# FFN chunks 2 to 10: first product made transposed, with weight blocks as stationary operands, and x^T scaled by the norm's factor

## The chip, the cores and the metric

One core of a Trainium2 chip runs the whole network. The metric is the device time of one launch in microseconds (us), the median of several runs. The engines named below are PE (matrix product; PEld is its weight load), DVE (vector), ACT (scalar), POOL and SP (which issues the weight DMAs). PE, ACT, DVE and POOL each run their own instructions in a fixed order and wait for one another by semaphores.

## What is computed

256 tokens of width 1024 pass through a first block of 4 layers and a second block of 2 layers. The FFN is the same gated product everywhere; there are 8 in the first block and 2 in the second, each with 2816 hidden values:

```python
def rms_norm(x, g, eps=NORM_EPS):
    xf = x.astype(jnp.float32)
    y = xf * lax.rsqrt(jnp.mean(xf * xf, axis=-1, keepdims=True) + eps)
    return (y * g.astype(jnp.float32)).astype(x.dtype)

def swiglu(x, w_in, w_out):
    gate, up = jnp.split(x @ w_in, 2, axis=-1)
    return (jax.nn.silu(gate) * up) @ w_out

    for i in range(DEPTH):
        g = norm_g[i]
        h = h + 0.5 * rms_norm(swiglu(rms_norm(h, g[0]), ffn_w_in[i, 0], ffn_w_out[i, 0]), g[1])
        m = rms_norm(h, g[2])
...
        h = h + rms_norm(m, g[3])
        h = h + 0.5 * rms_norm(swiglu(rms_norm(h, g[4]), ffn_w_in[i, 1], ffn_w_out[i, 1]), g[5])
```

The dots stand for an attention: differential in layers 0 and 3, causal in layer 1, and a three-branch one in layer 2. The second block's layers have a mixer and an FFN each, with norms that are shifted and scaled.

## The kernel before

The 256 tokens are two token tiles (t0 and t1) of 128 partitions, `h[0]` and `h[1]`. The network is 16 stages: in the first block FFN, attention, FFN for each layer (stages 0 to 11), then mixer and FFN twice (12 to 15). The ten FFNs are stages 0, 2, 3, 5, 6, 8, 9, 11, 13 and 15.

**Weights.** All weights are float32 and are read once. SP brings them as 128x2048 tiles `raw` (two buffers). Each is split (`hilo`) into a rounded part hi (ACT, CAST, L168) and a rest lo (DVE, subtraction, L169), in 128x1024 tiles, nine buffers of each. The activations are split in the same way, and a product is three matmuls (`mm3`): xh with wh (L217), xh with wl (L219), xl with wh (L221).

**An FFN** (`ffn`) goes over 11 chunks of 256 hidden columns. For a chunk c and a token tile t, `f1(c, t)` makes [tokens, 256 gate | 256 up] in one PSUM bank: `project`, 8 k-tiles of 3 matmuls, in which the stationary operand is a 128x128 block of x^T and the moving one is 512 columns of weights. `hidden` makes tanh (ACT, L411), the two products (DVE, L413, L414), and then `to_hT`: two PE transposes (L249), a cast (ACT, L261), a subtraction (DVE, L262). `f2(c, t)` multiplies these hidden values by rows of the second weight, into the accumulators aA (for t0) and aB (for t1), two banks each, 12 matmuls of 512 columns for a chunk and a token tile. The second product runs two chunks behind the first; after chunk 10 chunks 8, 9 and 10 are left for t0, then for t1.

**Between FFNs.** `finish` makes the sum of squares of the accumulator (ACT, L312; POOL, L313, L314), a power (POOL, L304), and adds to h (DVE, L379, L380). Then `prep` makes x^T for the next stage: the norm's factor r (again Square, L313, L314, L304) and, of it, r/2 and r^2 (POOL, L334, L335); the transposes of h (L249, two groups of four for each token tile); and with the norm's gain xh (ACT, L351) and xl (DVE, L352). The transposes take h as it is; r enters later, as r/2 in the tanh and as r^2 in L414. For the second block `prep_2` scales h by r on ACT (L1113) ahead of its transposes.

**Order.** Steps that hop between engines are generators that yield a number of us of PE's products, after which the next step is written; the framework then orders each engine's instructions by its own priorities, so that a group of transposes can stand between matmuls of another product.

Of the kernel before, what the change touches and what calls it, by code (L numbers as in the profile page):

```python
# [99 lines left out]
class _Net:  # L100
# [63 lines left out]
    # A float32 value is the exact sum of two float32r parts, hi and lo.  x @ w is taken as  # L164
    # xh @ wh + xh @ wl + xl @ wh, accumulated in float32.
# [69 lines left out]
    def out_step(self, acc, hT, ws, first, last, halves=(0, 1)):  # L235
        for k in range(2):
            x = ([hT[0][:, i] for i in range(2)], [hT[1][:, i] for i in range(2)])
# [3 lines left out]
    def last_steps(self, acc, steps):  # L241
        """steps: (hT, ws); one half of the columns after the other"""
# [8 lines left out]
    def to_hT(self, nat, scale=None):  # L251
        """[128 tok, 256] -> (hi, lo) [128, 2, 128 tok]."""
# [13 lines left out]
        return hi, lo  # L266

# [1 line left out]
    def setup(self):  # L269
# [13 lines left out]
        def columns(src, rows, eng=nc.sync):  # L283
            """DRAM [rows, 128] -> [128, rows]."""
# [14 lines left out]
        self.xT = [tuple(self.t(self.xp, [P, KT, P], f"x{n}{t}", F32R) for n in "hl") for t in range(NT)]  # L299

# [5 lines left out]
    def mean_square(self, halves, a0, a1):  # L306
        """a0 + a1 * the sum of squares of two [128, 512]; a1 is a number, a0 a number or [128, 1]"""
# [12 lines left out]
    def rstd(self, r, x):  # L320
        """r = (mean square of x [128, 1024] + eps) ^ -1/2"""
        self.powmh(r, self.mean_square(self.halves(x), EPS, 1.0 / D))

    def prep(self, t, li, slot):
        """x^T of the token tile with the norm's gain; gives the norm's factor per token (and
        half of it, and its square), which stays out of the products."""
        nc = self.nc
        h = self.h[t]
        fs = self.t(self.sp, [P, 3], f"fs{t}", bufs=2)

        def factors():
# [9 lines left out]
        yield 3.0 * t if initial else PREP_0  # L341
# [13 lines left out]
        if initial:  # L355
            factors()
        return fs
# [6 lines left out]
    def post_norm(self, t, acc, g_bc, a=1.0, eps=EPS):  # L364
        """h += acc * (a * mean square of acc + eps) ^ -1/2 * g"""
# [17 lines left out]
    def prepare(self, n, t):  # L383
        """Starts what the next part of the network needs of a token tile."""
# [12 lines left out]
    def ffn(self, w_in, w_out, factors, finish, middle):  # L397
# [3 lines left out]
        hT, wi, wo, acc = {}, {}, {}, {}  # L401

        def f1(c, t):
            self.prepared(t)
            if c not in wi:
                wi[c] = self.load_in(w_in, [(c * FC, FC), (DFF + c * FC, FC)])
            self.start(hidden(c, t, self.project(t, wi[c], 2 * FC)))

        def hidden(c, t, ps):
            th = self.t(self.fp, [P, FC], "th")  # L410
            nc.scalar.activation(th, ps[:, :FC], AF.Tanh, scale=factors(t)[0])  # L411
            hd = self.t(self.fp, [P, FC], "hd", bufs=3)
# [17 lines left out]

        first = ((0, 0), (0, 1), (1, 0), (1, 1)) if self.stage == 0 else ((0, 0), (1, 0), (0, 1), (1, 1))
# [17 lines left out]
    def ffn_1(self, li, j):  # L449
# [14 lines left out]
        self.ffn(self.a["ffn_w_in"][li, j], self.a["ffn_w_out"][li, j], factors, finish, middle)  # L464

# [1 line left out]
    def rope(self, x, nh, t):  # L467
        """first 16 of 64 dims of nh heads of x [128, nh, 64], in place"""
# [24 lines left out]
    def softmax(self, s, n, l):  # L493
        """s: PSUM [128, n, l] -> exp(s/8 - max) [128, n, l] and sums [128, n]"""
# [21 lines left out]
    def masked_scores(self, parts, dg):  # L516
        """parts: (psum slice, q^T, k^T) of a bank; dg: psum [128, n, 128], the diagonal blocks"""
# [11 lines left out]
    def qkv_layer(self, kind, w_in, w_out, li):  # L529
        """diff (kind 0) or plain causal (kind 1: with 256 tokens the one block of 256 is every  # L530
        query's own and none is left to select) attention."""
# [38 lines left out]
        def heads(j, t, pairs, last):  # L570
            """A group of pairs of 64-wide heads (or of diff heads of 2 components)."""
# [884 lines left out]
```

## Time and profile before

| | |
|---|---|
| runs | 2869.83, 2873.69, 2874.76 us |
| median | 2873.69 us |
| profiled execution, span | 2868.0 us |
| PE busy | 2823.5 us, 98%, 13373 matmuls |
| DVE, ACT, POOL busy | 66%, 53%, 8% |
| DMA | 549.32 MB, mean 192 GB/s |
| PE clock granted (mean) | 0.999 of full |

The span runs from the first to the last instruction of the profiled execution; the page gives no other time for that execution, and the median of the runs is 5.7 us above the span. On the page, an engine's share is its busy time by the span; the chain of waits is followed back from the last instruction; a row of the timeline is a start, a duration, the engine, the line, and the operation with output and inputs, and a bracket gives the idle time ahead of it and what ended it. A matmul's duration is longer than the distance to the next one, since they are pipelined, so distances of starts are used where PE's time is counted.

### The profile page before, as it was taken

What the parts mean: (1) busy time and instruction counts of PE and PEld (TensorE: products, weight loads), DVE (VectorE), ACT (ScalarE), POOL (GpSimd) and SP (SyncE); (2) the same over time, 40 slices, a digit from 0 to 9 for tenths busy, and PEclk for the clock granted to TensorE, in tenths of its full rate; (3) what the DMA queues carried; (4) which work ended last, traced back from release to release, by engine and by line L of the source; (5) the groups of instructions that cost most, each with busy time, mean ns of one, the idle gap of its engine ahead of it and who ended that gap; (6) DMA issues with size and microseconds to landing.
All of it is one profiled execution on the core that took longest, in us unless ns stands there. A gap on an engine that the chain in (4) does not pass through costs nothing.

```text
span 2868.0 us, 36025 instructions
## 1 busy us (share of the span) xinstructions
PE 2823.5 (98%) x13373; PEld 2311.4 (81%) x13373; DVE 1879.8 (66%) x2913; ACT 1509.0 (53%) x2655; POOL 231.5 (8%) x441
## 2 busy tenths in 40 slices
PE   8999999999999999999999999999999999999998
PEld 6887788888888888878888888778778888788787
DVE  6565767656466765656767666675676686675854
ACT  5456644545664454557545546654545544554543
POOL 0011200101110010020100001110001000000000
PEclk9999999999999999999999999999999999999999
DMA  7554567555446755552666555365565586564753
GB/s 236 186 181 157 171 219 243 179 188 187 157 158 217 249 182 180 191 157 74 222 211 220 194 181 188 128 227 191 187 203 201 172 294 202 192 223 168 236 182 126
DMA packets 356755, 549.32 MB, mean 192 GB/s; under 512 B 13890, under 2 KB 270772, under 8 KB 356580
## 3 DMA queue, kind: packets, MB, share of 16 engines
q1 hardware_dynamic: 354964, 542.00, 57.5%
q0 software_dynamic: 1248, 4.41, 0.4%
q8 instruction: 105, 1.72, 0.2%
q14 instruction: 70, 0.57, 0.1%
q10 hardware_dynamic: 368, 0.62, 0.1%
HBM read 545.93 MB, written 1.05 MB: 191 GB/s over the span
## 4 chain that ended last, share of the span: by engine, by line
PE 84%; ACT 4%; DVE 4%; DMA 4%; POOL 2%; issue 1%; SPq 0%; POOLq 0%; ACTq 0%; DVEq 0%
PE mm L221 18%; PE mm L217 17%; PE mm L219 17%; PE aA L217 4%; PE aA L219 4%; PE aA L221 4%; PE tp L249 4%; PE aB L221 3%; PE aB L217 3%; PE aB L219 3%; DVE lo L169 2%; ACT hi L168 1%; DMA raw<-in_ffn_w_in_dram 1%; DMA raw<-in_w_in_dram 1%; ACT junk L312 1%
## 5 line engine op out<-in xcount | busy, mean ns | idle before, releaser
L169 DVE TENSOR_TENSOR lo<-raw,hi 128x1024 fp32r<-128x1024 f32 x914 | 1102.1, 1221 | 668.1 <-ACT hi L168 655.7
L168 ACT CAST hi<-raw 128x1024 fp32r<-128x1024 f32 x914 | 942.8, 1049 | 927.6 <-PE mm L221 318.9
L217 PE MATMUL mm<-hi,xh 128*128 128x512 f32 (+2 forms) x2496 | 1005.2, 403 | 5.7 <-ACT hi L168 4.0
L221 PE MATMUL mm<-hi,xl 128*128 128x512 f32 (+2 forms) x2496 | 976.7, 392 | 4.3 <-DVE xl L352 4.3
L219 PE MATMUL mm<-lo,xh 128*128 128x512 f32 (+2 forms) x2496 | 973.0, 390 | 0.5 <-DVE lo L169 0.5
L221 PEld LDWEIGHTS mm<-hi,xl 128*128 128x128 f32 x2496 | 469.0, 188 | 108.6 <-DVE xl L352 8.1
L217 PEld LDWEIGHTS mm<-hi,xh 128*128 128x128 f32 x2496 | 469.7, 188 | 94.0 <-ACT hi L168 4.4
L219 PEld LDWEIGHTS mm<-lo,xh 128*128 128x128 f32 x2496 | 470.6, 189 | 87.6 <-DVE lo L169 1.0
L217 PE MATMUL aA<-hi,hT 128*128 128x512 f32 x584 | 194.1, 397 | 2.3 <-DVE on L631 2.3
L219 PE MATMUL aA<-lo,hT 128*128 128x512 f32 x584 | 190.6, 390 | 0.0
L221 PE MATMUL aA<-hi,hT 128*128 128x512 f32 x584 | 190.1, 391 | 0.0
L217 PE MATMUL aB<-hi,hT 128*128 128x512 f32 x568 | 188.8, 395 | 0.0
L221 PE MATMUL aB<-hi,hT 128*128 128x512 f32 x568 | 185.7, 390 | 0.8 <-DVE hT L265 0.8
L219 PE MATMUL aB<-lo,hT 128*128 128x512 f32 x568 | 186.0, 390 | 0.0
L313 POOL TENSOR_SCALAR s<-s 128x1 f32<-128x1 f32 x58 | 35.5, 611 | 1401.6 <-ACT junk L312 1400.9
L262 DVE TENSOR_TENSOR hT<-tp,hT 128x256 fp32r<-128x256 f32 x268 | 111.3, 419 | 27.0 <-ACT hT L261 26.1
L221 PEld LDWEIGHTS aA<-hi,hT 128*128 128x128 f32 x584 | 109.6, 188 | 23.4
L217 PEld LDWEIGHTS aA<-hi,hT 128*128 128x128 f32 x584 | 108.2, 188 | 24.6 <-issue 3.4
L219 PEld LDWEIGHTS aA<-lo,hT 128*128 128x128 f32 x584 | 109.7, 188 | 22.6
L261 ACT CAST hT<-tp 128x256 fp32r<-128x256 f32 x268 | 97.2, 367 | 55.7 <-PE tp L249 55.2
L221 PEld LDWEIGHTS aB<-hi,hT 128*128 128x128 f32 x568 | 106.6, 188 | 24.0 <-DVE hT L265 1.2
L217 PEld LDWEIGHTS aB<-hi,hT 128*128 128x128 f32 x568 | 106.4, 188 | 22.9 <-ACT P L503 1.3
(250 smaller groups left out, 2444.6 us busy)
## 6 DMA issues: line engine op xcount, KB each, us to landing
raw<-in_ffn_w_in_dram SPq DMA_DIRECT2D x352, 512.0 KB, 4.9
raw<-in_ffn_w_out_dram SPq DMA_DIRECT2D x88, 1024.0 KB, 5.0
raw<-in_w_in_dram SPq DMA_DIRECT2D x44, 1024.0 KB, 5.2
raw<-in_w_ffn_in_dram SPq DMA_DIRECT2D x88, 512.0 KB, 5.0
araw<-in_w_ada_dram SPq DMA_DIRECT2D x40, 1024.0 KB, 5.6
raw<-in_w_ffn_out_dram SPq DMA_DIRECT2D x22, 1024.0 KB, 5.0
raw<-in_diff_w_in_dram SPq DMA_DIRECT2D x32, 512.0 KB, 4.5
raw<-in_nsa_w_in_dram SPq DMA_DIRECT2D x9, 1024.0 KB, 5.1
```

The source lines that it names most:

```text
L168: self.nc.scalar.copy(hi, raw)
L169: self.nc.vector.tensor_tensor(lo, raw, hi.bitcast(F32), op=ALU.subtract)
L217: mm(ps, xh[k], wh[:, c], start=first, stop=False)
L219: mm(ps, xh[k], wl[:, c], start=False, stop=False)
L221: mm(ps, xl[k], wh[:, c], start=False, stop=last)
L249: self.nc.tensor.transpose(dst, src, self.ident[:k, :k])
L261: nc.scalar.copy(hi, v)
L262: nc.vector.tensor_tensor(lo, v, hi.bitcast(F32), op=ALU.subtract)
L312: nc.scalar.activation(junk, halves[i], AF.Square, accum_out=ss[:, i : i + 1])
L313: nc.gpsimd.tensor_scalar(v[:, 0:1], ss[:, 0:1], a1, a0, op0=ALU.mult, op1=ALU.add)
```

## The change

It does the following:

1. In each FFN, the chunks 2 to 10 go through `f1_T` instead of `f1`. A chunk is four `section`s: 128 gate columns, 128 up columns, the next 128 gate columns, the next 128 up columns, each for all 256 tokens. A section has, for each of 8 k-tiles, one matmul with a 128x128 block of wh as stationary operand that moves xh and xl of all tokens side by side (512 columns, L430), and one with a block of wl that moves xh (256 columns, L431). ACT copies the xl half out of PSUM (L434), DVE adds the other half (L435). The hidden values come out transposed, so `to_hT` with its transposes and its cast from PSUM is gone; `hilo` splits them from SBUF. Chunks 0 and 1 go as before.
2. `x2` is one tile that holds xh and xl of both token tiles.
3. For an FFN of the first block, `prep` scales h by r (ACT, L338, 128x512, two per token tile) into a tile `res` and transposes that. r/2 and r^2 are gone, and so are the factors in L411 and L414.
4. In stage 0, r was made after the transposes; now it is made ahead of them there too.

```diff
-    def prep(self, t, li, slot):
+    def prep(self, t, li, slot, scaled):
...
-        fs = self.t(self.sp, [P, 3], f"fs{t}", bufs=2)
-        def factors():
-            r = fs[:, 0:1]
-            self.rstd(r, h)
-            nc.gpsimd.tensor_scalar(fs[:, 1:2], r, 0.5, None, op0=ALU.mult)
-            nc.gpsimd.tensor_tensor(fs[:, 2:3], r, r, op=ALU.mult)
-        initial = self.clock == 0
-        if not initial:
-            factors()
+        r = self.t(self.sp, [P, 1], f"fs{t}", bufs=2)
+        self.rstd(r, h)
...
         for q in range(2):
+            if scaled:
+                xn = self.t(self.fp, [P, 512], "res", bufs=2)
+                nc.scalar.activation(xn, h[:, 512 * q : 512 * q + 512], AF.Copy, scale=r)
+            else:
+                xn = h[:, 512 * q : 512 * q + 512]
             tp = self.ps("tp")
             for k in range(4):
-                self.transpose(tp[:, k * P : k * P + P], h[:, (4 * q + k) * P : (4 * q + k + 1) * P])
+                self.transpose(tp[:, k * P : k * P + P], xn[:, k * P : k * P + P])
...
         def hidden(c, t, ps):
-            nc.scalar.activation(th, ps[:, :FC], AF.Tanh, scale=factors(t)[0])
-            nc.vector.scalar_tensor_tensor(hd, hd, factors(t)[1], ps[:, FC:], op0=ALU.mult, op1=ALU.mult)
+            hd = gate(ps)
             yield 4.0
             hT[c, t] = self.to_hT(hd)
+        def section(c, b, i):
+            ws = weights_in(c)
+            ps = self.ps("mm")
+            cs = slice(i * FC + b * P, i * FC + b * P + P)
+            for k in range(KT):
+                mm(ps, ws[k][0][:, cs], self.x2[:, k], start=k == 0, stop=False)
+                mm(ps[:, :S], ws[k][1][:, cs], self.x2[:, k, 0], start=False, stop=k == KT - 1)
+                self.spend(0.33)
+            r = self.t(self.mp, [P, S], "gu", bufs=3)
+            nc.scalar.copy(r, ps[:, S:])
+            nc.vector.tensor_tensor(r, ps[:, :S], r, op=ALU.add)
+            return r
+        def f1_T(c, b):
+            g = section(c, b, 0)
+            nc.scalar.activation(th, g, AF.Tanh, scale=0.5)
+            nc.vector.scalar_tensor_tensor(g, th, 1.0, g, op0=ALU.add, op1=ALU.mult)
+            hd = section(c, b, 1)
+            nc.vector.tensor_tensor(hd, hd, g, op=ALU.mult)
+            hi, lo = (self.t(self.xp, [P, 2, P], "hT", F32R, bufs=16) for _ in range(2))
+            self.hilo(hd, *(v.rearrange("p a b -> p (a b)") for v in (hi, lo)))
...
         for c in range(2, NCH):
-            for t in range(NT):
-                f1(c, t)
+            for i in range(2):
+                f1_T(c, i)
                 if c < NCH - 1:
-                    f2(c - 2, t=t)
+                    f2(c - 2, t=i)
```

The order of the instructions moves in three places. First, PE within a chunk, in stage 0. Before, the first product of a chunk for t1, with transposes of hidden values (`hd`) among its matmuls; the moving operand is named first, the stationary one second:

```order
303 L221 MATMUL mm_787<-hi_709,xl_15_100 128x512
304 L217 MATMUL mm_787<-hi_713,xh_14_99 128x512
305 L219 MATMUL mm_787<-lo_714,xh_14_99 128x512
306 L221 MATMUL mm_787<-hi_713,xl_15_100 128x512
307 L249 MATMUL tp_797<-cst_76,hd_762 128x128 x2
308 L217 MATMUL mm_787<-hi_713,xh_14_99 128x512
```

Now the end of one section and the start of the next, of a chunk in stage 0:

```order
207 L430 MATMUL mm_552<-x_12_97,hi_548 128x512
208 L431 MATMUL mm_552<-x_12_97,lo_549 128x256
209 L430 MATMUL mm_552<-x_12_97,hi_548 128x512
210 L431 MATMUL mm_552<-x_12_97,lo_549 128x256
211 L430 MATMUL mm_575<-x_12_97,hi_533 128x512
212 L431 MATMUL mm_575<-x_12_97,lo_534 128x256
```

The transposes are gone, and each block of weights is loaded as stationary operand, so all four tile pairs of a chunk (here hi_533 to hi_548) are read in every section.

Second, PE between the FFNs of stages 2 and 3, for t0. Before, the first group of transposes of h stands behind 21 of the 36 matmuls into aB that follow the last into aA, the second group behind 24:

```order
2131 L221 MATMUL aB_3428<-hi_4526,hT_4546 128x512
2132 L249 MATMUL tp_4614<-cst_76,h_2_78 128x128 x4
2133 L217 MATMUL aB_3428<-hi_4530,hT_4546 128x512
2134 L219 MATMUL aB_3428<-lo_4531,hT_4546 128x512
2135 L221 MATMUL aB_3428<-hi_4530,hT_4547 128x512
2136 L249 MATMUL tp_4630<-cst_76,h_2_78 128x128 x4
2137 L217 MATMUL aB_3429<-hi_4516,hT_4431 128x512
```

Now, with the scaled tile `res` as the source:

```order
2389 L217 MATMUL aB_3657<-hi_4924,hT_4762 128x512
2390 L249 MATMUL tp_5011<-cst_76,res_5009 128x128 x4
2391 L249 MATMUL tp_5029<-cst_76,res_5027 128x128 x4
2392 L219 MATMUL aB_3657<-lo_4925,hT_4762 128x512
2393 L221 MATMUL aB_3657<-hi_4924,hT_4763 128x512
```

Both groups now stand behind 28 of the 36, and 8 matmuls are left between them and the next FFN's first product.

Third, ACT at the start of the program (stage 0, t0 is h_2, t1 is h_3). Before, xh (L351) of the first k-tiles stood ahead of the first weight cast. Now:

```order
5 L314 ACTIVATE junk_102,s_14_100<-h_2_78 128x512
6 L314 ACTIVATE junk_104,s_14_100<-h_2_78 128x512
7 L314 ACTIVATE junk_112,s_19_110<-h_3_79 128x512
8 L168 CAST hi_155<-raw_152 128x1024
9 L314 ACTIVATE junk_114,s_19_110<-h_3_79 128x512
10 L338 ACTIVATE res_122<-h_2_78,fs_13_99 128x512
11 L338 ACTIVATE res_137<-h_2_78,fs_13_99 128x512
12 L168 CAST hi_159<-raw_152 128x1024
13 L349 ACTIVATE x_12_97<-tp_124,col_7_85 128x128
```

The scaling of t0 (L338) stands behind the first weight cast, and xh (now L349) behind the second.

## Rows read from the trace of the kernel before

**Rows 1.** The page: busy time, share, instructions of three engines.
```profile
PE 2823.5 (98%) x13373; PEld 2311.4 (81%) x13373; DVE 1879.8 (66%) x2913; ACT 1509.0 (53%) x2655; POOL 231.5 (8%) x441
```
**Rows 2.** The page: the chain that ended last, by engine.
```profile
PE 84%; ACT 4%; DVE 4%; DMA 4%; POOL 2%; issue 1%; SPq 0%; POOLq 0%; ACTq 0%; DVEq 0%
```
**Rows 3.** Busy time by stretch: a plain chunk, one with extra DVE work (stage 2).
```profile
core 0: us, PE busy (x) PEld busy (x) DVE busy (x) ACT busy (x) POOL busy (x), PEclk, DMA share, GB/s
...
398.40:415.20 16.80, 16.80 (x77) 13.85 (x76) 9.51 (x13) 7.64 (x10) 0.00 (x0) 1.00 0.60 189
...
448.90:465.70 16.80, 16.80 (x76) 13.76 (x76) 15.94 (x24) 7.90 (x10) 0.00 (x0) 1.00 0.90 307
```
**Rows 4.** PE's timeline in a chunk: start, duration, line, operation.
```profile
151.82 0.39 PE L221 MATMUL mm<-hi,xl 128*128 128x512 f32 x1
152.05 0.38 PE L249 MATMUL tp<-cst,hd 128*128 128x128 f32 x2
152.19 0.48 PE L217 MATMUL mm<-hi,xh 128*128 128x512 f32 x1
152.50 0.39 PE L219 MATMUL mm<-lo,xh 128*128 128x512 f32 x1
```
**Rows 5.** Timeline of PE and its loads: 256-column matmuls (stage 7).
```profile
1308.36 0.28 PE L221 MATMUL mm<-hi,xl 128*128 128x256 f32 x1
1308.36 0.19 PEld L217 LDWEIGHTS mm<-hi,xh 128*128 128x128 f32 x1
...
1308.48 0.28 PE L217 MATMUL mm<-hi,xh 128*128 128x256 f32 x1
...
1309.44 0.28 PE L221 MATMUL mm<-hi,xl 128*128 128x256 f32 x1
```
**Rows 6.** Groups by shape, ACT and DVE: busy us, mean ns, idle before.
```profile
L563 ACT COPY kT<-tp 128x256 f32<-128x256 f32 x24 | 8.9, 372 | 0.3
...
L262 DVE TENSOR_TENSOR hT<-tp,hT 128x256 fp32r<-128x256 f32 x268 | 111.3, 419 | 27.0 <-ACT hT L261 26.1
```
**Rows 7.** Timeline between the FFNs of stages 2 and 3.
```profile
508.69 0.62 PE L217 MATMUL aB<-hi,hT 128*128 128x512 f32 x2
...
513.45 0.60 PE L249 MATMUL tp<-cst,h 128*128 128x128 f32 x4
...
514.66 1.11 POOL L314 TENSOR_SCALAR s<-s,s 128x1 f32<-128x1 f32 x1
...
515.86 0.55 POOL L304 TENSOR_TENSOR fs<-s,cst 128x1 f32<-128x1 f32 x1
...
520.05 0.39 PE L219 MATMUL mm<-lo,xh 128*128 128x512 f32 x1
...
520.92 0.50 PE L221 MATMUL mm<-hi,xl 128*128 128x512 f32 x1 [0.48 <-DVE xl L352]
```
**Rows 8.** Timeline between stages 11 and 12, where h is scaled first.
```profile
2071.42 0.72 ACT L1113 ACTIVATE res<-h,s 128x512 f32<-128x512 f32 x1 [2.10 <-POOL s L304]
...
2072.19 0.66 PE L249 MATMUL tp<-cst,res 128*128 128x128 f32 x4 [2.02 <-ACT res L1113]
```
**Rows 9.** Groups by shape, PE: transposes of plain and of scaled h.
```profile
L249 PE MATMUL tp<-cst,h 128*128 128x128 f32 x192 | 29.9, 279 | 0.7 <-DVE h L380 0.7
...
L249 PE MATMUL tp<-cst,res 128*128 128x128 f32 x64 | 10.4, 285 | 7.7 <-ACT res L1113 7.7
```
**Rows 10.** Groups by shape: xh on ACT and xl on DVE.
```profile
L351 ACT ACTIVATE xh<-tp,col 128x128 fp32r<-128x128 f32 x192 | 62.6, 366 | 16.4 <-DVE xl L352 13.7 <-PE tp L249 2.2
...
L352 DVE SCALAR_TENSOR_TENSOR xl<-tp,col,xh 128x128 fp32r<-128x128 f32 x192 | 60.2, 345 | 9.8 <-ACT xh L351 9.0
```
**Rows 11.** Timeline of the start of the program.
```profile
9.46 0.55 POOL L304 TENSOR_TENSOR fs<-s,cst 128x1 f32<-128x1 f32 x1
...
10.81 1.04 ACT L168 CAST hi<-raw 128x1024 fp32r<-128x1024 f32 x1 [1.36 <-DMA raw<-in_ffn_w_in_dram]
...
11.91 0.79 PE L217 MATMUL mm<-hi,xh 128*128 128x512 f32 x1 [3.99 <-ACT hi L168]
```

More of the change, by code (lines that the diff above doesn't have):

```diff
@@ L236, in out_step @@
         for k in range(2):
-            x = ([hT[0][:, i] for i in range(2)], [hT[1][:, i] for i in range(2)])
+            x = hT
             self.mm3([(acc[i], slice(512 * i, 512 * i + 512)) for i in halves], x, k, ws[k],
@@ L265, in to_hT @@
             nc.vector.scalar_tensor_tensor(lo, v, scale, hi.bitcast(F32), op0=ALU.mult, op1=ALU.subtract)
-        return hi, lo
+        return [hi[:, i] for i in range(2)], [lo[:, i] for i in range(2)]
     def setup(self):
@@ L298, in setup @@
         self.cst = cst
-        self.xT = [tuple(self.t(self.xp, [P, KT, P], f"x{n}{t}", F32R) for n in "hl") for t in range(NT)]
+        self.x2 = self.t(self.xp, [P, KT, 2, S], "x2", F32R)
+        self.xT = [tuple(self.x2[:, :, i, t * P : t * P + P] for i in range(2)) for t in range(NT)]
     def powmh(self, dst, src):
@@ L322, in rstd @@
         self.powmh(r, self.mean_square(self.halves(x), EPS, 1.0 / D))
-    def prep(self, t, li, slot):
+    def prep(self, t, li, slot, scaled):
         nc = self.nc
         h = self.h[t]
-        fs = self.t(self.sp, [P, 3], f"fs{t}", bufs=2)
-        def factors():
-            r = fs[:, 0:1]
-            self.rstd(r, h)
-            nc.gpsimd.tensor_scalar(fs[:, 1:2], r, 0.5, None, op0=ALU.mult)
-            nc.gpsimd.tensor_tensor(fs[:, 2:3], r, r, op=ALU.mult)
-        initial = self.clock == 0
-        if not initial:
-            factors()
+        r = self.t(self.sp, [P, 1], f"fs{t}", bufs=2)
+        self.rstd(r, h)
         xh, xl = self.xT[t]
-        yield 3.0 * t if initial else PREP_0
+        yield 3.0 * t if self.clock == 0 else PREP_0
         for q in range(2):
+            if scaled:
[3 more added lines that the diff above has]
+                xn = h[:, 512 * q : 512 * q + 512]
             tp = self.ps("tp")
             for k in range(4):
-                self.transpose(tp[:, k * P : k * P + P], h[:, (4 * q + k) * P : (4 * q + k + 1) * P])
+                self.transpose(tp[:, k * P : k * P + P], xn[:, k * P : k * P + P])
             for k in range(4):
@@ L354, in prep @@
             yield PREP_1
-        if initial:
-            factors()
-        return fs
+        return r
     def gain_bc(self, src, tag=""):
@@ L394, in prepared, with ffn, weights_in, gate @@
         return self.ready[self.stage, t]
-    def ffn(self, w_in, w_out, factors, finish, middle):
+    def ffn(self, w_in, w_out, finish, middle):
         nc = self.nc
         hT, wi, wo, acc = {}, {}, {}, {}
+        def weights_in(c):
+            if c not in wi:
+                wi[c] = self.load_in(w_in, [(c * FC, FC), (DFF + c * FC, FC)])
+            return wi[c]
+        def gate(ps):
+            th = self.t(self.fp, [P, FC], "th")
+            nc.scalar.activation(th, ps[:, :FC], AF.Tanh, scale=0.5)
+            hd = self.t(self.fp, [P, FC], "hd", bufs=3)
+            nc.vector.scalar_tensor_tensor(hd, th, 1.0, ps[:, :FC], op0=ALU.add, op1=ALU.mult)
+            nc.vector.tensor_tensor(hd, hd, ps[:, FC:], op=ALU.mult)
+            return hd
@@ L403, in f1 @@
         def f1(c, t):
             self.prepared(t)
-            if c not in wi:
-                wi[c] = self.load_in(w_in, [(c * FC, FC), (DFF + c * FC, FC)])
-            self.start(hidden(c, t, self.project(t, wi[c], 2 * FC)))
+            self.start(hidden(c, t, self.project(t, weights_in(c), 2 * FC)))
         def hidden(c, t, ps):
-            th = self.t(self.fp, [P, FC], "th")
-            nc.scalar.activation(th, ps[:, :FC], AF.Tanh, scale=factors(t)[0])
-            hd = self.t(self.fp, [P, FC], "hd", bufs=3)
@@ L413, in hidden @@
-            nc.vector.scalar_tensor_tensor(hd, th, 1.0, ps[:, :FC], op0=ALU.add, op1=ALU.mult)
-            nc.vector.scalar_tensor_tensor(hd, hd, factors(t)[1], ps[:, FC:], op0=ALU.mult, op1=ALU.mult)
+            hd = gate(ps)
             yield 4.0
             hT[c, t] = self.to_hT(hd)
+        def section(c, b, i):
+            mm = nc.tensor.matmul
+            ws = weights_in(c)
[8 more added lines that the diff above has]
+            nc.vector.tensor_tensor(r, ps[:, :S], r, op=ALU.add)
+            return r
@@ new lines, in f1_T @@
+        def f1_T(c, b):
+            g = section(c, b, 0)
+            th = self.t(self.fp, [P, FC], "th")
+            nc.scalar.activation(th, g, AF.Tanh, scale=0.5)
[4 more added lines that the diff above has]
+            self.hilo(hd, *(v.rearrange("p a b -> p (a b)") for v in (hi, lo)))
+            for t in range(NT):
+                held.setdefault((c, t), ([], []))
+                for v, x in zip(held[c, t], (hi, lo)):
+                    v.append(x[:, t])
+                if b == 1:
+                    hT[c, t] = held[c, t]
@@ L429, in f2 @@
                 self.out_step(acc[t], *steps[0], cs[0] == 0, False)
+        held = {}
         first = ((0, 0), (0, 1), (1, 0), (1, 1)) if self.stage == 0 else ((0, 0), (1, 0), (0, 1), (1, 1))
@@ L635, in heads @@
             oT[j, t] = self.to_hT(on, None if kind == 1 else self.subcol[li])
-        rs[0] = self.prepared(0)[:, 0:1]
+        rs[0] = self.prepared(0)
         do_v(0, 0)
         do_qk(0, 0)
-        rs[1] = self.prepared(1)[:, 0:1]
+        rs[1] = self.prepared(1)
         do_v(0, 1)
@@ L939, in heads @@
             oT[g, t] = self.to_hT(on)
-        rs[0] = self.prepared(0)[:, 0:1]
+        rs[0] = self.prepared(0)
         c0(0)
         c12(0, 0)
-        rs[1] = self.prepared(1)[:, 0:1]
+        rs[1] = self.prepared(1)
         c0(1)
@@ L1132, in ffn_2 @@
         g = []
-        self.ffn(self.a["w_ffn_in_2"][l], self.a["w_ffn_out_2"][l], lambda t: (0.5, 1.0),
+        self.ffn(self.a["w_ffn_in_2"][l], self.a["w_ffn_out_2"][l],
                  lambda t, acc: self.gate_finish(g[0])(t, acc), lambda: g.append(self.start_gate(l, 5)))
@@ L1398, in run @@
                     body = lambda li=li: self.nsa_layer(li)
-                add(lambda t, li=li, part=part: self.prep(t, li, 2 * part), body, part == 1)
+                add(lambda t, li=li, part=part: self.prep(t, li, 2 * part, part != 1), body, part == 1)
         for l in range(DEPTH_2):
```

5 lines of the change are left out of this document (1 added, 4 removed).

## The prediction, made before the change was run

> **What bounds the kernel now.** I read the page's shares first: PE is busy 98% of the span, DVE 66%, ACT 53% [rows 1]. The chain that ended last agrees: 84% of it is PE, and the other 16% is spread over ACT, DVE, DMA and POOL [rows 2]. So time is gained by giving PE less to do, and lost wherever PE has to wait. Next, busy time by stretch: in a plain FFN chunk PE is busy all of 16.80 us, with DVE at 9.51 and ACT at 7.64, and even in a chunk in which DVE has 15.94 us of work PE does not wait [rows 3]. Then the timeline, for what one matmul costs: the reader should take distances of starts, not durations. Last, the places where PE does wait: between stages [rows 7, 8] and at the start [rows 11].
>
> The sum is made against the profiled execution, span 2868.0 us, for which the page gives no time around the span. The median of the runs, 2873.69, is 5.7 us above it, and I carry that distance over.
>
> **The chunk.** A matmul that moves 512 columns takes 0.23 us from start to start (151.82 to 152.05), and a pair of transposes adds about as much as one of them: from 152.05 to 152.50 are one pair and one matmul, 0.45 [rows 4]. A chunk of 16.8 us has 72 matmuls and two pairs, so a slot is 16.84/74 = 0.2275 us. Matmuls that move 256 columns, each with a new stationary block, start 0.120 us apart: nine steps from 1308.36 to 1309.44 take 1.08 [rows 5].
> Removed from a chunk: 48 x 0.2275 + 2 x 0.227 = 11.37 us. Added: 32 x 0.2275 + 32 x 0.120 = 11.12 us (four sections, 8 k-tiles, one matmul of each width). PE saves 0.25 to 0.27 us a chunk. There are 9 such chunks in each of 10 FFNs, 90 in all: **-24 us**. No row shows the two widths in turn. If the step of a 256-column matmul were half of a 512-column slot, 0.114, a chunk would save 0.45 and all 90 would give -41; if the turn cost 2 ns a matmul, 64 x 90 x 0.002 = 11.5 us would be lost, and -12 left. I take -24, since both steps are measured in long series.
>
> What else is added in a chunk lies beside PE. ACT's tanh stays, its cast of hidden values too; four copies of 128x256 from PSUM come, 0.372 each [rows 6]: 1.5 us on 7.64 of 16.6. DVE gets four additions, at most 0.419 each, and stays with its other operations: 1.7 us on 9.51 [rows 3, 6]. The cover is thin only in the chunks with extra DVE work: 15.94 + 1.7 is 17.6 us in a period of 16.6, one us too much. Such a chunk stands beside lighter ones, and weights are made about a chunk ahead, so I cost it at nothing. Without that cover each such chunk loses 1 us.
> The order of the hidden values is safe: the second product runs two chunks behind. POOL loses r/2 and r^2, off the path: nothing.
>
> **Between stages: seven FFNs of the first block (2, 3, 5, 6, 8, 9, 11).** Before, the transposes of h came as soon as h did: PE runs them at 513.45 without idle time [rows 7], and over all 192 transposes of h PE idled 0.7 us [rows 9]. PE's one loss there is at 520.92, 0.87 after the matmul before instead of 0.23: 0.64 us, waiting for xl [rows 7].
> Now the transposes wait for the norm's factor and the scaling. By the trace of before the factor is there at 515.86 + 0.55 = 516.41 [rows 7], and the scaling takes 0.72 [rows 8]: 517.2 with the hand-overs. PE, by the new order, is at the transposes after 28 of the 36 matmuls into aB: 508.69 + 28 x 0.2275 = 515.06 [rows 7]. It waits **2.1 us**. The same chain stands in the kernel already, ahead of the mixer: the transposes of scaled h waited 2.02 us there [rows 8], and 7.7 us over four such stages [rows 9].
> Behind this wait stands more. The second group waits for the second scaling, 0.3. Then only 8 matmuls, 1.8 us, are left before the next FFN, which starts at about 520.0. Its operands are made one by one, 0.366 for xh on ACT and 0.345 for xl on DVE [rows 10], the two halves in turn, with a weight cast of 1.04 [rows 11] among them. The first is there at about 519.3, but the second to fourth of the first half are each 0.6 to 1.5 us late, of which the matmuls of chunk 1, laid between in the order, hide a part: 0.7 here. For t1 the same chain, from a later h, costs 0.9 by my count. So 2.1 + 0.3 + 0.7 + 0.9 = 4.0, less the 0.64 of before: 3.4. Bounds: 1.3 (only the wait seen ahead of the mixer, 7.7/4 = 1.9, less 0.64) and 5. Seven times 3.4: **+24 us**, between +9 and +35. I take the inner value, as its largest term is the one that two stretches show.
>
> On this chain POOL's two scalar steps take long where DVE subtracts weights beside them: L314 took 1.11 us [rows 7]. The Trainium skill, "SBUF — State Buffer", on the shared port pair, says that a DVE operation with two SBUF inputs and a GpSimd (POOL) operation that reads SBUF block one another for a whole instruction. By that, these steps are as slow in the changed kernel, and would be quick only where no weight arrives; the sum does not change.
>
> **The start.** Before, x^T of t0 was made from plain h while the weights were on their way, and the first matmul waited for the first weight cast alone: 11.91 [rows 11]. Now ACT runs the Square of t1 and the scaling behind that cast, which begins at 10.81, then a second cast, then xh: 10.81 + 1.04 + 0.8 (half a Square, taken as the scaling of the same shape and a hand-over) + 2 x 0.72 + 1.04 + 0.37 = 15.5 [rows 8, 10, 11]. **+4 us**, 3 to 6, as the following operands come late too. The factor itself, which was there at 9.46 + 0.55 = 10.01 [rows 11], is not what is late.
>
> **Sum.** -24 + 24 + 4 = +4 us: span 2872, median **2878**. A measurement of this kernel tells about 0.2% (5.7 us) from no change, so the likeliest is "no change, slightly slower".
>
> **Rivals.**
> *Faster: the boundaries are mostly hidden.* The framework orders around the waits, as chunk 1's matmuls between chunk 0's show; then only the T wait remains, 7 x 1.3 = 9, and -24 + 9 + 4 = -11: 2863; with the cheaper 256-column step, 2846. For it: the neighbouring stage lost 1.9 and not 4 in that wait [rows 9]. Against: transposes in groups of four cannot be moved ahead of their data. Chance 0.28.
> *Slower: PE waits in the boundaries as much as my upper bound.* 7 x 5 = 35, start 6, and the turn of widths costs a little (-18): +23, 2897. It decides if xh and xl are as late as ACT's order makes them. Chance 0.20.
> *Slower: weights come late.* Every section reads all four tile pairs of its chunk, so they come free only during the last section, 2.8 us, while before they came free over 5.4. With nine buffers, the fourth pair of the next chunk waits for that; the cast (1.04) and the subtraction must be done before the next chunk's seventh k-tile, some 4.8 us later by the count of matmuls. That holds; if a stall of 0.5 us came in each chunk, 90 x 0.5 = 45: 2923. For it: the DMA share of 0.90 in a heavy chunk [rows 3]. Chance 0.09.
> *Slower: loads show.* The change makes 64 loads of 128 columns for the first product of a chunk where 48 and four small ones were. A load takes 0.19 us, starts with the matmul before it, and does not widen the 0.120 step [rows 5]. If 12 more loads each showed, 12 x 90 x 0.19 = +205: 3080. The Trainium skill, "TensorE: Matmul & The Clock Gate", Part 3 ("What overlaps and what doesn't"), says that a load overlaps a running matmul only if it targets other row groups, which these do not. By that, the loads would show, before as after; the trace does not agree. Chance 0.02.
>
> **How the numbers follow.** The forecast's own case has 0.41 and a range of its own of 2868 to 2890; it is split over "same" (most) and "slower". Faster by over 0.2%: the first rival, 0.28, and little more. Slower by over 0.2%: 0.31 from the three slower rivals and a part of the forecast's own case, 0.39 together. Same: 0.33. The range goes from inside the first rival's two values to the second rival's: 2855 to 2898.
>
> **What would show it.** In a chunk of the changed kernel PE should be busy throughout, with a period of 16.55 to 16.6 us, and matmuls 0.23 and 0.12 us apart in turn; a longer period or idle time in PE means the third or fourth rival. Between FFNs the row of transposes of `res` should show about 2 us of idle time for each stage, released by ACT's scaling, and xh and xl should then release matmuls; under 10 us over the seven stages means the first rival. The first matmul should be at about 15.5. The forecast is wrong if the chunk's period is under 16.4 or over 16.75, or if all boundaries together lose less than 15 or more than 35 us over before.

## The result and the profile after

The changed kernel took 2915.73 us (median of 4 runs, 2911.56 to 2917.11) where the kernel before took 2871.88 (4 runs of the same session, 2869.83 to 2874.76). The ratio is 1.0153, with a 95% interval of 1.0139 to 1.0168: 44 us slower. I had forecast 2878 with a range of 2855 to 2898. The profiled execution of the change has a span of 2915.3 us, 47 us more than the one before.

Engine loads on the page of the change, against [rows 1]:

```profile
PE 2837.9 (97%) x14453; PEld 2362.2 (81%) x14453; DVE 1987.0 (68%) x3273; ACT 1625.3 (56%) x3047; POOL 227.8 (8%) x393
```

PE was busy for 14 us longer, where I had taken 24 us from it, and its idle time grew by about 33 us. So two things went wrong: PE's busy time did not fall, and PE waits. The groups by shape of PE say where. They show busy us, mean ns, and idle time before with what ended it:

```profile
L430 PE MATMUL mm<-x,hi 128*128 128x512 f32 x2880 | 1024.9, 398 | 2.1 <-DVE gu L435 2.1
L431 PE MATMUL mm<-x,lo 128*128 128x256 f32 x2880 | 808.2, 281 | 0.0
...
L249 PE MATMUL tp<-cst,res 128*128 128x128 f32 x192 | 35.8, 319 | 46.2 <-ACT res L338 38.4 <-ACT res L1147 7.8
```

The transposed chunks hardly wait: 2.1 us in 2880 pairs of matmuls. The transposes of scaled h wait 38.4 us for ACT's new scaling (L338), where those of plain h waited 0.7 [rows 9]; the 7.8 for L1147 are the second block's, 7.7 before [rows 9].

Now the steps in a chunk, PE's timeline, against [rows 4, 5]:

```profile
399.76 0.28 PE L431 MATMUL mm<-x,lo 128*128 128x256 f32 x1
399.88 0.40 PE L430 MATMUL mm<-x,hi 128*128 128x512 f32 x1
400.12 0.28 PE L431 MATMUL mm<-x,lo 128*128 128x256 f32 x1
400.24 0.40 PE L430 MATMUL mm<-x,hi 128*128 128x512 f32 x1
400.47 0.28 PE L431 MATMUL mm<-x,lo 128*128 128x256 f32 x1
400.58 0.40 PE L217 MATMUL aA<-hi,hT 128*128 128x512 f32 x1
```

Take distances of starts: 399.88 to 400.12 and 400.24 to 400.47 for the 512 columns, 400.12 to 400.24 for the 256. Over all pairs of the trace the 512-column step ahead of a 256-column matmul has a median of 0.236 us (0.227 where another 512 follows) and the 256-column step one of 0.117. A pair takes 0.353 us, not 0.3475.

What a chunk takes as a whole is the distance between the first matmuls of the second product for t0 (L217, aA) in two chunks that follow one another. Two such starts in the kernel before, and the one that follows 400.58 in the change:

```profile
392.47 0.62 PE L217 MATMUL aA<-hi,hT 128*128 128x512 f32 x2
409.32 0.62 PE L217 MATMUL aA<-hi,hT 128*128 128x512 f32 x2
```

```profile
417.36 0.63 PE L217 MATMUL aA<-hi,hT 128*128 128x512 f32 x2
```

That is 16.85 us before and 16.78 now (16.77 in most plain chunks of the trace). A chunk saves about 0.08 us, not 0.25 to 0.27, and 90 chunks about 8 us, not 24. The prediction had named a period over 16.75 as a sign that it is wrong.

Then the boundary of stages 2 and 3, against [rows 7]. PE's timeline:

```profile
525.07 1.27 PE L249 MATMUL tp<-cst,res 128*128 128x128 f32 x8 [2.06 <-ACT res L338]
...
539.97 1.11 PE L249 MATMUL tp<-cst,res 128*128 128x128 f32 x4 [2.54 <-ACT res L338]
540.74 0.78 PE L219 MATMUL mm<-lo,x 128*128 128x512 f32 x1
541.31 0.63 PE L221 MATMUL mm<-hi,x 128*128 128x512 f32 x1
541.74 1.05 PE L249 MATMUL tp<-cst,res 128*128 128x128 f32 x4
```

Two waits, one for each token tile; here that of t1 is the longer. Over the seven boundaries t0 waits 2.2 us in the mean (1.75 to 2.90) and t1 2.4 (1.72 to 2.57). Together that is 31.9 us; the wait at the start, 6.5, makes it 38.4. The same stretch on POOL, then on DVE, says why t1's factor is late:

```profile
526.29 0.19 POOL L315 TENSOR_SCALAR s<-s 128x1 f32<-128x1 f32 x1 [2.03 <-ACT junk L314]
530.60 0.26 POOL L316 TENSOR_SCALAR s<-s,s 128x1 f32<-128x1 f32 x1 [4.12 <-ACT junk L314]
...
536.16 1.99 POOL L316 TENSOR_SCALAR s<-s,s 128x1 f32<-128x1 f32 x1 [1.67 <-ACT junk L314]
538.23 0.93 POOL L306 TENSOR_TENSOR fs<-s,cst 128x1 f32<-128x1 f32 x1
```

```profile
535.08 2.35 DVE L169 TENSOR_TENSOR lo<-raw,hi 128x1024 fp32r<-128x1024 f32 x2
537.35 1.41 DVE L1063 SCALAR_TENSOR_TENSOR ada<-araw,col,ada 128x512 f32<-128x512 f32 x2
```

The operation that POOL does in 0.26 us at 530.60, for the norm of the accumulator and with DVE idle, takes 1.99 at 536.16, while DVE runs weight subtractions and accumulations from SBUF one behind the other, and the power step behind it takes 0.93. Ahead of stage 2 it is the step before (L315) that is slow, on POOL and then DVE:

```profile
338.70 3.79 POOL L315 TENSOR_SCALAR s<-s 128x1 f32<-128x1 f32 x1 [3.61 <-ACT junk L314]
338.95 3.48 DVE L169 TENSOR_TENSOR lo<-raw,hi 128x1024 fp32r<-128x1024 f32 x3
```

In six of t1's seven chains one of these two steps took 2.0 to 3.8 us.

Busy time by stretch adds something that I had not looked for. The columns are as in [rows 3]; the last but two is the granted clock of PE:

```profile
521.00:523.00 2.00, 2.00 (x9) 1.32 (x8) 2.00 (x3) 1.10 (x4) 1.44 (x2) 1.00 0.00 0
...
527.00:529.00 2.00, 2.00 (x6) 1.54 (x5) 1.42 (x3) 1.21 (x3) 0.00 (x0) 0.50 0.86 303
541.00:543.00 2.00, 2.00 (x8) 1.62 (x8) 0.35 (x1) 0.90 (x3) 0.00 (x0) 0.50 0.60 210
545.00:547.00 2.00, 2.00 (x10) 1.65 (x10) 2.00 (x6) 1.01 (x3) 0.00 (x0) 1.00 0.00 0
```

After each of the two waits PE ran at half its clock (0.50, 1.2 GHz of 2.4) for some 3 us: 6 matmuls in the 2 us from 527 where 9 or 10 are usual, and the steps from 540.74 to 541.31 and from there to 541.74 are 0.57 and 0.43 us. The trace of the change holds 34 us of such stretches between the start and the end, that of before none. About 24 us of them stand at seven of the fourteen waits of the seven boundaries, from shortly before their end or after it. The others are 3.4 us behind a wait ahead of stage 12 and 6.8 us in stage 7, at 1366 us, behind no wait over 0.4 us.

The start, ACT's timeline and then PE's, against [rows 11]:

```profile
9.90 1.04 ACT L168 CAST hi<-raw 128x1024 fp32r<-128x1024 f32 x1 [1.24 <-DMA raw<-in_ffn_w_in_dram]
...
11.48 1.32 ACT L338 ACTIVATE res<-h,fs 128x512 f32<-128x512 f32 x2
```

```profile
12.24 1.97 PE L249 MATMUL tp<-cst,res 128*128 128x128 f32 x8 [6.50 <-ACT res L338]
14.05 0.80 PE L217 MATMUL mm<-hi,x 128*128 128x512 f32 x1
```

The scaling stands behind the first cast, as the order said. The weights landed 0.9 us earlier in this execution, and measured from that cast the first matmul comes 4.15 us later where it came 1.10 us later before.

### The profile page after: what moved, and what is told of

Same layout as the page of the kernel before. It is cut to its first block, busy times and chain, and to the rows that moved or that the text cites. A ratio compares the mean times of both kernels' runs of the same rounds, so it can differ in the third digit from the quotient of the medians.

```text
span 2915.3 us, 38810 instructions
## 1 busy us (share of the span) xinstructions
PE 2837.9 (97%) x14453; PEld 2362.2 (81%) x14453; DVE 1987.0 (68%) x3273; ACT 1625.3 (56%) x3047; POOL 227.8 (8%) x393
## 4 chain that ended last, share of the span: by engine, by line
PE 51%; DMA 4%; DVE 3%; ACT 3%; POOL 2%; issue 1%; POOLq 0%; DVEq 0%; ACTq 0%; SPq 0%
PE mm L430 13%; PE mm L431 7%; PE mm L221 4%; PE mm L219 4%; PE mm L217 4%; PE aA L217 3%; PE aA L219 3%; PE aA L221 3%; PE tp L249 2%; PE aB L219 2%; PE aB L217 2%; PE aB L221 2%; DMA raw<-in_w_in_dram 2%; DVE lo L169 1%; ACT hi L168 1%
## 5 line engine op out<-in xcount | busy, mean ns | idle before, releaser
L430 PE MATMUL mm<-x,hi 128*128 128x512 f32 x2880 | 1024.9, 398 | 2.1 <-DVE gu L435 2.1
L431 PE MATMUL mm<-x,lo 128*128 128x256 f32 x2880 | 808.2, 281 | 0.0
L430 PEld LDWEIGHTS mm<-x,hi 128*128 128x128 f32 x2880 | 541.0, 188 | 134.8 <-DVE gu L435 3.6
L431 PEld LDWEIGHTS mm<-x,lo 128*128 128x128 f32 x2880 | 543.8, 189 | 6.9
L217 PE MATMUL mm<-hi,x 128*128 128x512 f32 (+2 forms) x1056 | 426.9, 405 | 2.1 <-ACT x L168 1.3
L221 PE MATMUL mm<-hi,x 128*128 128x512 f32 (+2 forms) x1056 | 415.4, 394 | 2.8 <-DVE x L350 2.7
L219 PE MATMUL mm<-lo,x 128*128 128x512 f32 (+2 forms) x1056 | 415.3, 394 | 0.0
L434 ACT COPY gu<-mm 128x256 f32<-128x256 f32 x360 | 132.5, 368 | 203.0 <-PE mm L431 202.9
L221 PEld LDWEIGHTS mm<-hi,x 128*128 128x128 f32 x1056 | 200.5, 190 | 49.6 <-DVE x L350 8.2
L217 PEld LDWEIGHTS mm<-hi,x 128*128 128x128 f32 x1056 | 200.7, 190 | 43.1 <-ACT x L349 4.1
L435 DVE TENSOR_TENSOR gu<-mm,gu 128x256 f32<-128x256 f32 x360 | 151.0, 420 | 123.3 <-ACT gu L434 122.7
L219 PEld LDWEIGHTS mm<-lo,x 128*128 128x128 f32 x1056 | 201.3, 191 | 34.7 <-issue 0.3
L217 PE MATMUL aA<-hi,hT 128*128 128x512 f32 x584 | 194.9, 398 | 3.0 <-DVE on L665 2.3
L217 PE MATMUL aB<-hi,hT 128*128 128x512 f32 x568 | 189.9, 397 | 0.2 <-ACT hT L264 0.2
```

The costliest lines, as they stand in the source:

```text
L217: mm(ps, xh[k], wh[:, c], start=first, stop=False)
L219: mm(ps, xh[k], wl[:, c], start=False, stop=False)
L221: mm(ps, xl[k], wh[:, c], start=False, stop=last)
L430: mm(ps, ws[k][0][:, cs], self.x2[:, k], start=k == 0, stop=False)
L431: mm(ps[:, :S], ws[k][1][:, cs], self.x2[:, k, 0], start=False, stop=k == KT - 1)
L434: nc.scalar.copy(r, ps[:, S:])
```

## The experiments

All are compared with the kernel before and the change. The kernel before was timed again in each set: its medians are 2869.96 us in the first (runs 1 to 4) and 2872.38 in the second (5 to 8). The change was not, so a difference to the change carries that spread of some 2 us; the ratios to before do not.

**1. x^T from plain h.** The change without the scaling, to see what the scaling costs. The norm's factor is left out of the FFNs of the first block altogether; all other work stays.

```diff
-                add(lambda t, li=li, part=part: self.prep(t, li, 2 * part, part != 1), body, part == 1)
+                add(lambda t, li=li, part=part: self.prep(t, li, 2 * part, False), body, part == 1)
```

> Leaves out the norm's factor r in the FFNs of the first block: x^T is made from plain h, everything else as in the change. Theory A (the loss is the wait of the transposes for the scaled h: 42 us of idle time ahead of them that the trace of the change shows over that of before, at seven boundaries and the start): the time falls by 38 to 46 us to about 2870 to 2878, and the transposes between FFNs show under 1 us of idle time. Rival B (the loss is in the transposed chunks or in the added ACT and DVE work): it stays above 2895.

Measured: 2873.63 us (2865.79 to 2877.47), ratio to before 1.0008 (0.9997 to 1.0019). The loss is gone. Groups by shape of PE:

```profile
L249 PE MATMUL tp<-cst,h 128*128 128x128 f32 x192 | 30.7, 283 | 3.8 <-DVE x L350 3.1 <-DVE h L376 0.7
```

The transposes of plain h wait 0.7 us for h, as before, and once, at the start, 3.1 for DVE's xl (L350), which reads what the transposes left in PSUM. Theory A holds. Yet the time is that of before: the transposed chunks, as the change makes them, gain nothing that the time shows. PE's busy and idle time say where the 8 us of the chunks went:

```profile
PE 2819.4 (98%) x14453; PEld 2353.9 (82%) x14453; DVE 1986.4 (69%) x3273; ACT 1607.0 (56%) x3015; POOL 219.2 (8%) x393
```

The span is 2867.8 us, so PE is busy 4.1 us less than before [rows 1] and idle 3.9 us more. Its chunks have the period of the change. But 6.8 us of this trace are at half clock, worth up to 3.4, and PE waits 5.3 us for xh (L349) where it waited 0.9 before.

**2. The scaling alone.** Chunks 2 to 10 made as before, x^T scaled.

```diff
-                f1_T(c, i)
+                f1(c, i)
```

> The scaling and the wide x^T tile stay, chunks 2 to 10 are made as before (tokens on the partitions, with transposes of the hidden values). Theory A: the scaling alone costs what the change costs, since the transposed chunks neither gain nor lose: 2910 to 2920, chunk period 16.85 us. Rival B: under 2890. If the transposed chunks do gain the 24 us of my prediction, it is above 2935.

Measured: 2914.36 us (2911.50 to 2915.59), ratio 1.0149 (1.0133 to 1.0164). Its transposes of `res` wait as in the change:

```profile
L249 PE MATMUL tp<-cst,res 128*128 128x128 f32 x192 | 33.1, 304 | 46.0 <-ACT res L338 38.1 <-ACT res L1147 7.9
```

With 1 this takes the change apart: the scaling costs all of the 44 us, and the transposed chunks neither cost nor bring anything that the time shows.

**3. The widths grouped.** In a section, all eight 512-column matmuls, then all eight 256-column ones.

```diff
             for k in range(KT):
                 mm(ps, ws[k][0][:, cs], self.x2[:, k], start=k == 0, stop=False)
-                mm(ps[:, :S], ws[k][1][:, cs], self.x2[:, k, 0], start=False, stop=k == KT - 1)
-                self.spend(0.33)
+                self.spend(0.22)
+            for k in range(KT):
+                mm(ps[:, :S], ws[k][1][:, cs], self.x2[:, k, 0], start=False, stop=k == KT - 1)
+                self.spend(0.11)
```

> Within a section all eight matmuls of 512 columns come first, then all eight of 256. Theory C (the turn from one width to the other costs: a 512-column matmul ahead of a 256-column one takes 0.236 us to the next start where 0.227 is usual): steps go back to 0.227 and 0.120, a chunk falls by about 0.2 us, the whole by 15 to 20 us to about 2896 to 2901. Rival D (the step is set by something else, such as the operands' places): steps and time stay, 2911 to 2917. The lo tiles come free later, so that new waits for weights could take some of it.

Measured: 2899.55 us (2892.35 to 2901.79), ratio to before 1.0094 (1.0077 to 1.0111); 16 us less than the change. PE's timeline, one section:

```profile
403.48 1.98 PE L430 MATMUL mm<-x,hi 128*128 128x512 f32 x8
405.29 1.11 PE L433 MATMUL mm<-x,lo 128*128 128x256 f32 x8
406.24 2.00 PE L430 MATMUL mm<-x,hi 128*128 128x512 f32 x8
```

405.29 - 403.48 = 1.81 us for eight, 0.226 each; 406.24 - 405.29 = 0.95, 0.119 each. A section takes 2.76 us, which is what I had reckoned (8 x 0.3475 = 2.78). The period of a chunk, by the same starts as above:

```profile
400.73 0.63 PE L217 MATMUL aA<-hi,hT 128*128 128x512 f32 x2
417.34 0.63 PE L217 MATMUL aA<-hi,hT 128*128 128x512 f32 x2
```

It is 16.61 us, what the prediction expected (16.55 to 16.6), where the change had 16.78. The operands and the number of loads are the same as in the change, so it is the turn of widths that cost 16 us (14 to 16 by the periods and steps). With the widths other things take turns too (blocks of wh and of wl, the whole PSUM bank and half of it), which no run takes apart, and why a 512-column step grows by 9 ns ahead of a 256-column one no run shows.

**4. Two scalar steps moved from POOL to DVE.** For the FFNs' factor alone; the power stays on POOL.

```diff
-        self.rstd(r, h)
+        if scaled:
...
+            nc.vector.tensor_scalar(v[:, 0:1], ss[:, 0:1], 1.0 / D, EPS, op0=ALU.mult, op1=ALU.add)
+            nc.vector.tensor_scalar(v[:, 1:2], ss[:, 1:2], 1.0 / D, v[:, 0:1], op0=ALU.mult, op1=ALU.add)
+            self.powmh(r, v[:, 1:2])
+        else:
+            self.rstd(r, h)
```

> The two scalar steps between the Square of h and the power are made on DVE instead of POOL, for the scaled parts alone. Theory E (POOL's steps are held by DVE's subtractions beside them: 0.88, 1.12, 1.99 us where 0.19 and 0.27 are usual): each of 14 chains becomes 1 to 2 us shorter, all together 14 to 24 us, to about 2892 to 2902. Rival F (DVE runs in order, so that the steps wait behind the same subtractions): no change, 2910 to 2918.

Measured: 2884.93 us (2879.63 to 2889.88), ratio to before 1.0046 (1.0033 to 1.0058); 31 us less than the change, more than theory E's 14 to 24. Groups by shape of PE, and DVE's timeline at the same boundary as above:

```profile
L249 PE MATMUL tp<-cst,res 128*128 128x128 f32 x192 | 31.7, 290 | 22.4 <-ACT res L347 14.9 <-ACT res L1156 7.4
```

```profile
529.49 0.15 DVE L337 TENSOR_SCALAR s<-s 128x1 f32<-128x1 f32 x1
529.56 1.22 DVE L169 TENSOR_TENSOR lo<-raw,hi 128x1024 fp32r<-128x1024 f32 x1
...
531.00 0.21 DVE L338 TENSOR_SCALAR s<-s,s 128x1 f32<-128x1 f32 x1
531.14 2.35 DVE L169 TENSOR_TENSOR lo<-raw,hi 128x1024 fp32r<-128x1024 f32 x2
```

On DVE the steps take 0.15 and 0.21 us, between the subtractions and not beside them. The power stayed on POOL, and in t1's chains it takes 1.46 us. The waits for ACT's scaling fell from 38.4 to 14.9 us, by 23.5, of which 3.0 at the start; other waits grew. The page tells what is left:

```profile
PE 2828.8 (98%) x14453; PEld 2352.2 (81%) x14453; DVE 1989.6 (69%) x3305; ACT 1626.1 (56%) x3047; POOL 203.9 (7%) x361
```

With a span of 2887.8 us PE's idle time is 59.0, 18.4 less than in the change, and its busy time is 9.1 less. The busy time fits the clock: with waits of about 1 us instead of 2 to 2.5, the trace holds 10 us at half clock instead of 34, none of them behind these waits, worth up to half of the difference, 12 us. That share is argued from the two traces; no run takes it by itself.

**5. Both cures.** 3 and 4 together.

> The change with grouped widths and with the scalar steps on DVE. If the two losses are independent, 2884.9 - 16 = 2869, between 2864 and 2874, no different from before. If the wait at the boundaries only takes up what the chunks gave back, above 2878.

Measured: 2870.37 us (2868.66 to 2876.19), ratio 0.9998 (0.9989 to 1.0008). The two losses are independent; 45 us are back. By the page PE is busy 2811.6 us of a span of 2866.9: 12 us less busy than before and 11 us more idle, so what the chunks save goes into the waits that are left. The granted clock of this execution, from the view by core:

```profile
core 0: 2866.9 us, clock 0.999
```

The change had 0.994 there; here it is that of the kernel before, 0.999.

**6. The factor as a row.** x^T of plain h. Where tokens lie along the free axis, r is needed as a row: 128 copies of r are transposed, and DVE multiplies twice for each half chunk. Chunks 0 and 1 take r/2 and r^2 as before; widths are grouped, and the tile `hd` has two buffers, not three.

```diff
+        nc.vector.tensor_scalar(rb, self.c["ident"], 0.0, r, op0=ALU.mult, op1=ALU.add)
...
+        self.transpose(tp[:, :P], rb)
+        nc.scalar.copy(self.rrow[:, t * P : t * P + P], tp[:, :P])
...
             g = section(c, b, 0)
+            if rows:
+                nc.vector.tensor_tensor(g, g, self.rrow, op=ALU.mult)
...
             nc.vector.scalar_tensor_tensor(g, th, 1.0, g, op0=ALU.add, op1=ALU.mult)
+            if rows:
+                nc.vector.tensor_tensor(g, g, self.rrow, op=ALU.mult)
```

> x^T of plain h as before the change; the norm's factor is made a row along the tokens (one transpose for each token tile) and multiplied in on DVE, twice for each half chunk (0.42 us each, 1.7 us a chunk); widths grouped. Theory: the boundaries cost what they did before, the chunks keep the gain: 2873.6 - 16 = 2857, between 2853 and 2864, faster than both. Rival: DVE becomes the bound in the chunks with extra DVE work (12.1 + 1.7 us and more in 16.6): 2866 or more, with PE waiting in those chunks.

Measured: 2857.83 us (2856.51 to 2862.47), ratio to before 0.9954 (0.9939 to 0.9968). This version beats both kernels: 0.46% under the one before. Page of it, then two of its chunks by stretch, one with more DVE work than the other:

```profile
PE 2812.3 (98%) x14469; PEld 2357.7 (83%) x14469; DVE 2096.9 (73%) x3577; ACT 1613.5 (56%) x3031; POOL 225.9 (8%) x425
```

```profile
437.00:453.60 16.60, 16.60 (x90) 14.32 (x89) 12.21 (x21) 8.59 (x15) 0.00 (x0) 1.00 0.48 161
...
470.00:486.50 16.50, 16.50 (x89) 14.26 (x88) 13.63 (x22) 10.01 (x16) 0.00 (x0) 1.00 0.66 203
```

DVE has 217 us more than before [rows 1] and PE still waits for nothing in these chunks; in the whole trace the sections wait 4.1 us for DVE, 2.1 in the change. Off the path, work on an engine with room costs next to nothing, whereas one 0.72 us scaling on the path [rows 8], with what it draws in behind the norm, cost 44.

**7. Two and two.** Two matmuls of 512 columns, then two of 256, in turn: a test of the turn by dose.

```diff
-            for k in range(KT):
-                mm(ps, ws[k][0][:, cs], self.x2[:, k], start=k == 0, stop=False)
-                mm(ps[:, :S], ws[k][1][:, cs], self.x2[:, k, 0], start=False, stop=k == KT - 1)
-                self.spend(0.33)
+            for k0 in range(0, KT, 2):
+                for k in (k0, k0 + 1):
+                    mm(ps, ws[k][0][:, cs], self.x2[:, k], start=k == 0, stop=False)
...
+                for k in (k0, k0 + 1):
+                    mm(ps[:, :S], ws[k][1][:, cs], self.x2[:, k, 0], start=False, stop=k == KT - 1)
```

> Two matmuls of 512 columns, then two of 256, in turn: half as many turns as the change, eight times as many as fully grouped less one. Theory C (a turn costs some 9 ns): 32 of 64 steps a chunk keep the usual 0.227 and 0.120, a gain of 7 to 10 us, 2906 to 2909. If the cost is not in the turns, 2914 to 2917 as the change, or 2900 as grouped.

Measured: 2903.83 us (2902.16 to 2907.03), ratio to before 1.0114 (1.0098 to 1.0131), 12 us less than the change, a little more than the 7 to 10 expected. The median steps of its trace are 0.233 for both 512-column places and 0.115 and 0.119 for the 256-column ones, 0.700 us for two pairs against 0.706 in the change and 0.694 grouped. They seem to lie half of the way. The period of a chunk says otherwise:

```profile
609.76 0.63 PE L217 MATMUL aA<-hi,hT 128*128 128x512 f32 x2
626.34 0.62 PE L217 MATMUL aA<-hi,hT 128*128 128x512 f32 x2
```

It is 16.58 us (16.59 in most plain chunks), where it is 16.61 grouped and 16.78 in the change. With half as many turns the whole loss of the chunk is back, so theory C, a price for each turn, does not hold: what costs is the strict turn, one and one. That 12 us and not 16 were gained in time is no sign of a dose either, as the intervals of the ratios of runs 3 and 7 overlap and the spans of their traces, 2899.5 and 2900.4 us, are 1 us apart.

**8. t1's transposes later.** Behind 45 matmuls of t0's first two chunks, not 32.

```diff
-        yield 3.0 * t if self.clock == 0 else PREP_0
+        yield 3.0 * t if self.clock == 0 else 9.5 if scaled and t else PREP_0
```

> The transposes of t1's scaled h are put behind 45 of the 48 matmuls of t0's first two chunks instead of 32. If t1's wait (2.7 us at each of seven boundaries) only lacked independent work, it goes: 2897 to 2902. Rival: with so few matmuls left, xh and xl of t1 are late instead, and the time goes to those waits: 2908 to 2916.

Measured: 2912.90 us (2907.94 to 2917.02), ratio to before 1.0142 (1.0126 to 1.0157): the rival's time, though not for its reason. The groups by shape of PE show where the wait went:

```profile
L249 PE MATMUL tp<-cst,res 128*128 128x128 f32 x192 | 32.1, 296 | 28.8 <-ACT res L338 21.5 <-ACT res L1147 7.2
...
L249 PE MATMUL tp<-cst,hd 128*128 128x128 f32 x80 | 15.7, 278 | 9.8 <-DVE hd L410 9.8
```

16.9 us went from the transposes of `res`, and 9.8 came back at transposes of hidden values, which stand there in PE's order now and wait for DVE; xh and xl of t1 are not late. Moving the place of a wait on PE did not shorten the chain that it waits for; 4 did.

## Why the prediction was wrong

The places were named, and the sign of each term was right. Two steps failed and took the time out of the range: the saving in the chunk was a third of what I put, and the clock stood in no term. A third, t1's wait, failed too but was made up by chance.

- **The chunk: "PE saves 0.25 to 0.27 us a chunk ... -24 us".** This step failed. I took both steps from long series of one width and had no row with the two in turn. In turn a pair takes 0.353 us and not 0.3475, 16 us over 2880 pairs; run 3 gives those 16 us back. My bound for this ("if the turn cost 2 ns a matmul", 11.5 us lost) was too small: it costs 2.8 ns a matmul. What is left of -24 is -8, as the period of the chunk shows. Run 1 has those chunks, and its time is still that of before: the 8 us went mostly to waits for xh and to half clock. That the 256-column step is 0.12 and the loads do not show was right.
- **The clock, in no step at all.** I reckoned every matmul at the steps of full clock. Waits of 1.7 to 2.9 us brought stretches at 1.2 GHz at seven of fourteen places, some 24 us at the boundaries; the whole trace holds 34 us, worth up to 17 us. How much of that the waits cause is argued from the traces, since some stretches stand behind no wait.
- **The wait for the scaled h, t0: "It waits 2.1 us".** Right: 2.06 at that boundary, 2.2 in the mean of the seven.
- **t1: "costs 0.9 by my count".** Wrong: 2.54 there, 2.4 in the mean. I counted t1's chain as t0's from a later h. DVE makes xl of t0 between the steps of t1's residual, and POOL's scalar steps, slow beside DVE, took 1.99 and 0.93 us instead of 1.12 and 0.62 for t0. I had seen L314 at 1.11 us [rows 7] and concluded that the sum does not change; it did, since that chain came to lie on the path twice at each boundary. Run 4 takes two of these steps off POOL and 23.5 us of waiting for the scaling with them.
- **The sum of the boundaries: "+24".** Its waits came out at 31.9 - 7 x 0.64 = +27 us, but by luck: the 0.3 for the second group and the 0.7 for late operands, 7 us in all, did not come (no wait for xh or xl over 0.4 us there), and t1's wait was 10 us more. With the half clock behind these waits, up to 12 us more, the boundaries pass the 35 us that the prediction had named as a sign that it is wrong.
- **The Trainium skill, "SBUF — State Buffer", on the shared port pair.** The trace agrees with what I cited of it: 0.26 us without such DVE work beside it, 1.99 with it, and quick again when done by DVE itself. I had weighed the rule and not used it: it spoke against putting this chain on the path.
- **The start: +4.** About right: the first tanh of the network starts at 25.11 us, where it was at 21.50, 3.6 us.
- **What hides: right within the chunks.** The four copies and four additions of a chunk cost PE 2.1 us of waits in the whole trace, and the chunks with extra DVE work do not wait; weights were not late and loads did not show, so rivals three and four fell. The second rival had the right place and too low a price.

Together, by the two spans, which are 47 us apart: chunks -8, start +4, waits at the boundaries +27, the clock up to +17. To these comes PE's idle time around stage 12, 4 us more than before, which the sum did not have; it differs from trace to trace (0.5 us more in run 2). That is 44 of the 47. Against the forecast of +4, the chunks make 16 of the difference and the clock up to 17. The first rival, that boundaries are mostly hidden, is refuted by run 2.

## What to carry to other kernels

Ahead of an operation that makes PE wait, follow the whole chain that it will hang on, for every tile, and reprice its small steps with what the neighbouring engines do at that time; a scalar step on POOL that is harmless off the path took 2 to 3.8 us on it. Apply a factor where there is room and nobody waits (6), not where it delays the first operand (2). A step measured in a series of equal matmuls is not the step in a mixed series: write equal widths together; two and two was enough here (3, 7).

## What the runs showed of the hardware

- Matmuls of 512 and 256 columns in turn take 0.236 and 0.117 us a step, grouped 0.227 and 0.120, with the same operands and as many loads. The period of a chunk is 16.78 us in turn, 16.61 grouped, and 16.58 two and two (the change, runs 3 and 7). The cause stays open.
- A POOL operation on 128x1 values (L315, L316 in the change) takes 0.19 to 0.27 us with DVE idle and up to 3.79 beside DVE operations with both inputs in SBUF.
- PE at half clock (0.50, 1.2 GHz) after idle time: in the change after the waits of 2.06 and 2.54 us. A wait can so cost some 1.5 us more than its idle time. But not every such wait brings it: in the change seven of the fourteen at the seven boundaries did, and the longest, 2.90 us at 1408.15, did not. After the wait of 2.02 us in the kernel before [rows 8] the granted clock stayed at 1.00, by the same view of that kernel:

```profile
2072.00:2074.00 2.00, 1.81 (x10) 1.59 (x11) 1.11 (x4) 2.00 (x5) 0.18 (x1) 1.00 1.01 393
```

  Run 5, with waits of 0.6 to 1.5 us at the boundaries, has no such stretch between the start and the end.
